# Products of probabilities with values for two heads at a time, in alternating column halves of TensorE

## The chip, the cores and the metric

The kernel runs on one core of a Trainium2 chip. A core has five engines that work beside each other: TensorE (PE, matrix products; its weight loads are shown apart as PEld), VectorE (DVE), ScalarE (ACT), GpSimd (POOL) and SyncE (SP, which here issues DMA transfers). TensorE writes only to PSUM, eight banks of 2 KB per partition; the other engines read from there. The metric is the device time of one execution in microseconds (us), the median of three runs.

## The reference

A forward pass of 512 tokens (and 256 context tokens) of width 1024 through two layers of a first block, each a mixer and a mixture of experts, and one layer of a second block. The change touches two mixers only. What they compute there is softmax attention with heads of 64:

```python
def gqa_attend(qb, k, v):
    s = jnp.einsum('bqhgd,bkhd->bhgqk', qb, k).astype(jnp.float32) * ATTN_SCALE
    p = jax.nn.softmax(s, -1)
    return jnp.einsum('bhgqk,bkhd->bqhgd', p.astype(v.dtype), v)
...
def sink_attend(qb, k, v, sink, valid=None):
    ...
    p = jax.nn.softmax(jnp.concatenate([s, sk], -1), -1)[..., :-1]
    return jnp.einsum('bhgqk,bkhd->bqhgd', p.astype(v.dtype), v)
...
def row_block(a):
    ...
    p = jax.nn.softmax(jnp.concatenate([s_nb, s_cx], -1), -1).astype(v.dtype)
    return (jnp.einsum('bhqk,bqkhd->bqhd', p[..., :n_nb], v_nb)
            + jnp.einsum('bhqk,bkhd->bqhd', p[..., n_nb:], vc))
```

The first is the first mixer's (2 groups of 4 heads, each group with one set of keys and values), the second the second mixer's window attention (2 groups of 4 heads again), the third its neighbourhood attention (8 heads). The last product of each, of the probabilities `p` with the values `v`, is what the change rearranges.

## The kernel before

All of it is float32. The projections and scores use float32r operands, split into a high and a low part; the transposes of the probabilities and their products with the values are plain float32, and in the trace each of these products leaves two matmul records.

**Stages that matter here.** In the first mixer (`mixer_ab`) `attend_gqa(u)` runs for the groups u = 4 and 5: 6 blocks of 128 queries times 4 heads. The two context blocks come first (256 keys, 2 blocks of keys), then four blocks with 768 keys (6 blocks of keys). In the second mixer (`mixer_cd`) `attend_window(g)` runs for g = 0 and 1: 4 blocks times 4 heads with 4 or 5 blocks of keys. Then `attend_near(u)` runs for u = 0 to 3: 4 column groups times 2 heads with 4 blocks of keys.

**One head.** `front` makes the scores `s` on TensorE (in PSUM, tag "s"), the negated maximum `nm` on VectorE, the exponential `p` and its sum on ScalarE, and multiplies `p` by the reciprocal of the sum on VectorE. `back` transposes `p` block by block on TensorE into `t` (PSUM, tag "aux"), three blocks to a tile, ScalarE copies each tile to `pT` in SBUF, and TensorE multiplies the 64 columns of values, as stationary operand, with each block of `pT` and accumulates in `po` (tag "aux" again). A head's 64 columns of values use half of the array's columns: the lower half for even heads, the upper for odd ones, and the result stands in partitions 0 to 63 or 64 to 127 of `po`. ScalarE then copies these 64 partitions to `oT`; where the result is the last one (u = 5, near u = 3) ScalarE writes the high part `oh` and VectorE the low part `ol`.

**What sets the order.** Each attention stage is a generator that yields once per head, and `both` takes steps of a second generator in between: the projection of the next group, or for u = 5 products of modulation rows and for near u = 3 nothing. Heads overlap by one: the front of the next head is written before the back of this one (near u = 3: three ahead). From this text a scheduler sets a fixed order for each engine, and every engine then goes through its list in that order. The tags "s", "mm" and "aux" of PSUM have two buffers each, so a new "aux" tile waits until the one before the last has been read.

**Other users.** The mixture of experts does its products in the same half-array form: `up` (line 1555) writes its two 64-row halves of `u` in turn, and the state products `pz` of the second block (line 2119) go to the two halves by turns too.

Of the kernel before, what the change touches and what calls it, by code (L numbers as in the profile page):

```python
# [13 lines left out]
F32 = mybir.dt.float32  # L14
# [3 lines left out]
AF = mybir.ActivationFunctionType  # L18
# [5 lines left out]
P = 128  # L24
# [146 lines left out]
class Kern:  # L171
# [276 lines left out]
    def scores_softmax(self, ap, ps, q, khl, k0, kn, tag, bufs):  # L448
# [12 lines left out]
        nc.scalar.activation(p[:, :kn], s[:, :kn], AF.Exp, bias=nm, accum_out=den)  # L461
        return p, den

    def probs_T(self, ap, ps, p, kn):
        nc = self.nc
        nk = kn // P
        pT = ap.tile([P, 6, P], F32, tag="pT", name="pT")
        for a in range(0, nk, 3):
            n = min(3, nk - a)
            t = ps.tile([P, 3, P], F32, tag="aux", name="t")  # L470
            for j in range(n):
                self.transpose(t[:, j], p[:, (a + j) * P:(a + j + 1) * P])
            nc.scalar.activation(pT[:, a:a + n], t[:, :n], AF.Copy)
        return pT
# [35 lines left out]
    def mixer_ab(self, atp, then):  # L510
        nc, tc, A, cp = self.nc, self.tc, self.A, self.cp
        NT, NB = NLAT + NCTX, 6
        with ExitStack() as es:
# [143 lines left out]
            def attend_diff(u):  # L657
                Q, Kh, Kl, V = ready[u]
                O = None
                oss = sp.tile([P, NB], F32, tag="oss", name="oss")  # L660

                def front(b):
                    k0, kn = keys(b)
                    (p0, d0), (p1, d1) = (self.scores_softmax(ap, ps, Q[:, c, b * P:(b + 1) * P], (Kh[:, c], Kl[:, c]), k0, kn,
                                                              f"p{c}", 2 - c) for c in range(2))
                    r0 = ap.tile([P, 1], F32, tag="r0", name="r0")
                    r1 = ap.tile([P, 1], F32, tag="r1", name="r1")
                    nc.vector.reciprocal(r0, d0)
                    nc.vector.tensor_scalar(p0[:, :kn], p0[:, :kn], r0, None, op0=OP.mult)
                    nc.vector.reciprocal(r1, d1)  # L670
                    nc.vector.tensor_mul(r1, r1, nlam)
                    nc.vector.scalar_tensor_tensor(p0[:, :kn], p1[:, :kn], r1, p0[:, :kn], op0=OP.mult, op1=OP.add)  # L672
                    return p0

                def back(b, p):
                    k0, kn = keys(b)
                    pT = self.probs_T(ap, ps, p, kn)
                    po = ps.tile([P, 512], F32, tag="aux", name="po")
                    for j in range(kn // P):
                        nc.tensor.matmul(po[:, :P], pT[:, j], V[:, k0 // P + j], start=j == 0, stop=j == kn // P - 1)  # L680
                    nc.scalar.activation(O[:, b], po[:, :P], AF.Copy)
                    nc.scalar.activation(po[:, P:2 * P], po[:, :P], AF.Square, accum_out=oss[:, b:b + 1])

                def norm():
                    v = sp.tile([P, NB], F32, tag="ov", name="ov")
                    nc.vector.tensor_scalar(v, oss, 1.0 / P, 1e-6, op0=OP.mult, op1=OP.add)
                    r = self.rsqrt(sp, v, NB)
                    for b in range(NB):
                        nc.vector.tensor_scalar_mul(O[:, b], O[:, b], r[:, b:b + 1])

                def out():
                    for b0 in (0, 3):
                        t = ps.tile([P, 3, P], F32, tag="aux", name="t")
                        for b in range(3):
                            self.transpose(t[:, b], O[:, b0 + b])
                        nc.scalar.activation(oT[:, u, b0 * P:(b0 + 3) * P], t, AF.Copy, scale=subg)

                p = front(0)
                while late:
                    late.pop(0)()  # L700
                O = sp.tile([P, NB, P], F32, tag="O", name="O", bufs=1)
                for b in range(NB):
                    nxt = front(b + 1) if b + 1 < NB else None
                    yield
                    back(b, p)
                    p = nxt
                late.extend((norm, out))

            def attend_gqa(u):
                Q, Kh, Kl, V = ready[u]  # L710
                order = (4, 5, 0, 1, 2, 3)

                def front(i):
                    b, h = order[i // 4], i % 4
                    k0, kn = keys(b)
                    p, den = self.scores_softmax(ap, ps, Q[:, h, b * P:(b + 1) * P], (Kh[:, 0], Kl[:, 0]), k0, kn, "p0", 2)
# [5 lines left out]
                def back(i, p):  # L722
                    b, h = order[i // 4], i % 4
# [6 lines left out]
                    rows, ch, tok = slice(o0, o0 + 64), 4 + (u - 4) * 2 + h // 2, slice(b * P, (b + 1) * P)  # L730
                    if u == 4:
                        nc.scalar.activation(oT[rows, ch, tok], po[rows, :P], AF.Copy)
                    else:
                        self.split(o[0][rows, ch, tok], o[1][rows, ch, tok], po[rows, :P])

                p = front(0)
                while late:
                    late.pop(0)()
                for i in range(4 * NB):
                    nxt = front(i + 1) if i + 1 < 4 * NB else None  # L740
                    yield
                    back(i, p)
                    p = nxt
                    if u == 5 and i % 4 == 0:
                        self.split(o[0][:, i // 4], o[1][:, i // 4], oT[:, i // 4])

            def last():
                yield from self.mod_rows(1, (1, 0), st, mp, ps, "mm", late=self.late)
# [31 lines left out]
    def mixer_cd(self, atp, then):  # L780
# [3 lines left out]
        with ExitStack() as es:  # L784
# [56 lines left out]
            def softmax(s, s0, s1, sinkcol, tag="p"):  # L841
                nm = ap.tile([P, 1], F32, tag="nm", name="nm", bufs=4)
                nc.vector.tensor_reduce(nm, s[:, s0:s1], axis=AX.X, op=OP.max, negate=True)
                if sinkcol is not None:
                    nc.vector.tensor_scalar(nm, nm, nsink[:, sinkcol:sinkcol + 1], None, op0=OP.min)
                p = ap.tile([P, 640], F32, tag=tag, name="p")
# [10 lines left out]
            def values(p, V, o0, wide=False):  # L857

                n = len(V)
                pT = ap.tile([P, 5, P], F32, tag="pT", name="pT")  # L860
# [7 lines left out]
                po = ps.tile([P, 512], F32, tag="aux", name="po")  # L868
                for j in range(n):
                    nc.tensor.matmul(po[o0:o0 + 64, :P], V[j], pT[:, j], start=j == 0, stop=j == n - 1)  # L870
                return po[o0:o0 + 64, :P]

            def project_window(g, Ws=()):
                QK = qp.tile([P, 3584], FR, tag="QK", name="QK")
# [32 lines left out]
            def attend_window(g):  # L907
# [18 lines left out]
                def back(i, p):  # L926
                    b, h = divmod(i, 4)
                    o0 = (h % 2) * 64
                    po = values(p, [V[:, j] for j in [*range(max(0, b - 1), min(4, b + 2)), 4, 5]], o0)
                    nc.scalar.activation(oT[o0:o0 + 64, g * 2 + h // 2, b * P:(b + 1) * P], po, AF.Copy)  # L930

                yield from piped(16, front, back)

            def project_near(u):
                c0 = u * P
# [54 lines left out]
            def attend_near(u):  # L990
# [19 lines left out]
                def back(i, p):  # L1010
                    g, h = divmod(i, 2)
                    hs = slice(h * 64, (h + 1) * 64)
                    po = values(p, [VW[:, g, 0, hs], VW[:, g, 1, hs], VX[:, 0, hs], VX[:, 1, hs]], h * 64, u == 3)
                    to = lambda t: t[hs, 4 + u, :NLAT].rearrange("p (r g i) -> p g r i", g=4, i=16)[:, g]
                    po = po.rearrange("p (r i) -> p r i", i=16)
                    if u < 3:
                        nc.scalar.activation(to(oT), po, AF.Copy)
                    else:
                        self.split(to(o[0]), to(o[1]), po)
                        if i < 7:  # L1020
                            self.split(o[0][:, i, :NLAT], o[1][:, i, :NLAT], oT[:, i])
# [1249 lines left out]

RAWS = 7

ORDER = [g * 8 + i for i in range(8) for g in range(4)]
# [81 lines left out]
```

## Time and profile before

| | us |
|---|---|
| median of 3 runs | 3471.41 |
| lowest, highest | 3470.51, 3473.18 |
| the profiled execution, whole | 3476.67 |
| its span, first to last instruction | 3474.9 |

The profile is of one execution. Its page gives each engine's busy time, and 40 slices of the span with the share of each engine in tenths. The first mixer's attention over u = 4 and 5 lies at 363 to 537 us, the second mixer's window and neighbourhood attention at 1365 to 1652 us. The trace can be asked for stretches, for lines of the kernel and for single instructions; the rows that are used stand two sections on. A matmul's record is longer than its place in the stream: matmuls are pipelined and a record includes the way through the array, so the pitch from start to start is the price of one, and a busy TensorE isn't one at its peak.

### The profile page before, as it was taken

What the parts mean: (1) busy time and instruction counts of PE and PEld (TensorE: products, weight loads), DVE (VectorE), ACT (ScalarE), POOL (GpSimd) and SP (SyncE); (2) the same over time, 40 slices, a digit from 0 to 9 for tenths busy, and PEclk for the clock granted to TensorE, in tenths of its full rate; (3) what the DMA queues carried; (4) which work ended last, traced back from release to release, by engine and by line L of the source; (5) the groups of instructions that cost most, each with busy time, mean ns of one, the idle gap of its engine ahead of it and who ended that gap; (6) DMA issues with size and microseconds to landing.
All of it is one profiled execution on the core that took longest, in us unless ns stands there. A gap on an engine that the chain in (4) does not pass through costs nothing. (4 is left out here: it accounts for less than half of the span.)

```text
span 3474.9 us, 50552 instructions
## 1 busy us (share of the span) xinstructions
PE 3146.0 (91%) x19045; PEld 2289.0 (66%) x19045; DVE 1479.0 (43%) x3317; ACT 1038.0 (30%) x2243; POOL 546.3 (16%) x533
## 2 busy tenths in 40 slices
PE   7999999799999938999799999569999999979998
PEld 3677767555555526887655555258798888858887
DVE  5578665521111147655622112154533333365533
ACT  4355562111111114655211111023223332233321
POOL 1101002141211111011232121220022210010000
PEclk9999999799999978999899999879999999989999
DMA  7433142699999641111499999552121212423332
GB/s 249 153 98 108 53 155 98 278 398 416 416 416 415 274 135 49 30 54 55 168 381 366 399 416 402 230 157 73 54 75 49 67 55 91 148 77 97 97 127 73
DMA packets 273506, 647.72 MB, mean 186 GB/s; under 512 B 58210, under 2 KB 176370, under 8 KB 223042
## 3 DMA queue, kind: packets, MB, share of 16 engines
q1 hardware_dynamic: 245522, 602.04, 46.5%
q0 software_dynamic: 26608, 38.36, 3.6%
q8 instruction: 187, 3.06, 0.4%
q10 hardware_dynamic: 1088, 3.42, 0.3%
q14 instruction: 101, 0.83, 0.1%
HBM read 670.51 MB, written 47.61 MB: 207 GB/s over the span
## 5 line engine op out<-in xcount | busy, mean ns | idle before, releaser
L1555 PE MATMUL u<-raw,xs 128*64 128x256 f32 x5376 | 602.1, 383 | 4.5 <-DMA raw<-in_k_w 4.1
L1555 PEld LDWEIGHTS u<-raw,xs 128*64 128x64 f32 x5376 | 381.9, 138 | 205.7 <-issue 15.0
L235 DVE TENSOR_TENSOR wl<-raw,wh 128x2048 fp32r<-128x2048 f32 (+4 forms) x176 | 273.7, 1561 | 430.1 <-ACT wh L234 428.6
L234 ACT ACTIVATE wh<-raw 128x2048 fp32r<-128x2048 f32 (+3 forms) x180 | 239.4, 1335 | 436.6 <-PE pm L229 187.9
L228 PE MATMUL pm<-hTh,wh 128*128 128x512 f32 x872 | 344.2, 395 | 1.9 <-DVE hTl L235 1.4
L230 PE MATMUL pm<-hTh,wl 128*128 128x512 f32 x872 | 340.9, 391 | 1.1 <-DVE wl L235 1.1
L229 PE MATMUL pm<-hTl,wh 128*128 128x512 f32 x872 | 341.2, 391 | 0.0
L1575 PE MATMUL y<-raw,gs 128*64 128x512 f32 x1344 | 305.0, 600 | 4.6 <-ACT gs L1570 2.1
L1560 DVE TENSOR_TENSOR sg<-sg,u 128x256 f32<-128x256 f32 x132 | 55.0, 420 | 498.5 <-PEq L1608 263.2
L1590 POOL DMA_INDIRECT y_d<-ys,rt_si x128 | 127.4, 995 | 716.9 <-issue 274.9
L228 PE MATMUL pm<-wh,aTh 128*128 128x384 f32 (+2 forms) x576 | 206.9, 360 | 8.0 <-ACT aTh L444 8.0
L230 PE MATMUL pm<-wh,aTl 128*128 128x384 f32 (+2 forms) x576 | 203.3, 353 | 4.0 <-POOL aTl L445 3.6
L1575 PEld LDWEIGHTS y<-raw,gs 128*64 128x64 f32 x1344 | 91.3, 137 | 171.8 <-issue 162.1
L229 PE MATMUL pm<-wl,aTh 128*128 128x384 f32 (+2 forms) x576 | 201.1, 350 | 2.1 <-DVE wl L235 2.1
L1559 ACT ACTIVATE sg<-u 128x256 f32<-128x256 f32 x132 | 50.6, 383 | 469.4 <-PE u L1555 298.0
L228 PEld LDWEIGHTS pm<-hTh,wh 128*128 128x128 f32 x872 | 163.6, 188 | 37.5 <-DVE hTl L235 1.8
L230 PEld LDWEIGHTS pm<-hTh,wl 128*128 128x128 f32 x872 | 163.3, 187 | 36.1 <-DVE wl L235 1.5
L229 PEld LDWEIGHTS pm<-hTl,wh 128*128 128x128 f32 x872 | 163.6, 188 | 34.4
L258 PE MATMUL t<-ident,p 128*128 128x128 f32 x704 | 127.5, 288 | 6.2 <-DVE p L672 1.1
L228 PEld LDWEIGHTS pm<-wh,aTh 128*128 128x128 f32 x576 | 115.4, 200 | 18.1 <-ACT aTh L444 11.2
L230 PEld LDWEIGHTS pm<-wh,aTl 128*128 128x128 f32 x576 | 115.0, 200 | 12.0 <-issue 4.9
L1582 DVE SCALAR_TENSOR_TENSOR ys<-y,rt_sw,gate 128x512 f32<-128x512 f32 x64 | 46.6, 749 | 178.2 <-PE y L1575 91.2
(557 smaller groups left out, 5583.9 us busy)
## 6 DMA issues: line engine op xcount, KB each, us to landing
raw<-in_k_w SPq DMA_DIRECT2D x408, 1024.0 KB
raw<-in_mod_w SPq DMA_DIRECT2D x192, 256.0 KB
raw<-in_w_in SPq DMA_DIRECT2D x16, 1024.0 KB
raw<-in_w_in SPq DMA_DIRECT2D x24, 512.0 KB
raw<-in_w_gate SPq DMA_DIRECT2D x12, 1024.0 KB
raw<-in_w_ff_gate SPq DMA_DIRECT2D x11, 1024.0 KB
raw<-in_w_ff_up SPq DMA_DIRECT2D x11, 1024.0 KB
raw<-in_w_ff_down SPq DMA_DIRECT2D x11, 1024.0 KB
```

The source lines that it names most:

```text
L228: nc.tensor.matmul(out, lh, rh, start=start, stop=False)
L229: nc.tensor.matmul(out, lh, rl, start=False, stop=False)
L230: nc.tensor.matmul(out, ll, rh, start=False, stop=stop)
L234: self.nc.scalar.activation(h, x, AF.Copy)
L235: (sub or self.nc.vector).tensor_sub(l, x, h)
L258: self.nc.tensor.transpose(out, in_, self.ident[:k, :k])
L1555: nc.tensor.matmul(pu[c][i][64 * n:64 * n + 64], xs[:, k, tok], w[:, k % 4, n * 256:(n + 1) * 256], start=k == 0, stop=k == KC - 1)
L1559: nc.scalar.activation(sg[c], pu[c][0], AF.Silu)
L1560: nc.vector.tensor_mul(sg[c], sg[c], pu[c][1])
L1575: nc.tensor.matmul(py[c][64 * n:64 * n + 64], gs[:, c, k % 2, k // 2], W[k // 2][:, k % 2, n * 512:(n + 1) * 512], start=k == 0, stop=k == 3)
L1582: nc.vector.scalar_tensor_tensor(y, py[c], sw, gate, op0=OP.mult, op1=OP.mult)
L1590: nc.gpsimd.indirect_dma_start(out=y_rows, out_offset=bass.IndirectOffsetOnAxis(ap=si, axis=0), in_=y, in_offset=None, bounds_check=4 * nt ...
```

## The change

The products of two heads are made together. `paired` replaces `piped` and the loop of `attend_gqa`: it keeps two fronts ahead, transposes one head per step (`turn`, `turned`, `probs_T`), and after each second head calls `back` with both transposed sets. The new `values` goes through the blocks of keys and issues for each block one product for the lower half and one for the upper half, both into one `po` tile, of which the lower 64 partitions belong to one head and the upper 64 to the other. So one copy (or one `oh` and one `ol`) of 128 partitions takes the place of two of 64. The tiles `pT` get 3 buffers in the first mixer (before 2) and 2 in the second as before; `p` alternates between two tags in `attend_gqa` with two buffers each, and has 3 buffers in the second mixer; near u = 3 goes from three fronts ahead to two.

```diff
+def paired(n, front, turn, back):
+
+    x, t = [front(i) for i in range(2)], []
+    for i in range(2 * n):
+        if i + 2 < 2 * n:
+            x.append(front(i + 2))
+        yield
+        t.append(turn(x.pop(0), i // 2))
+        if i % 2:
+            back(i // 2, t)
+            t = []
...
+    def values(self, po, parts):
+
+        n = len(parts[0][0])
+        for j in range(n):
+            for i, (V, pT) in enumerate(parts):
+                self.nc.tensor.matmul(po[64 * i:64 * i + 64], V[j], pT[:, j], start=j == 0, stop=j == n - 1)
...
-        pT = ap.tile([P, 6, P], F32, tag="pT", name="pT")
+        pT = ap.tile([P, 6, P], F32, tag="pT", name="pT", bufs=PT0)
...
-                                                              f"p{c}", 2 - c) for c in range(2))
+                                                              f"p{c}", 2) for c in range(2))
...
-                    pT = self.probs_T(ap, ps, p, kn)
                     po = ps.tile([P, 512], F32, tag="aux", name="po")
-                    o0 = (h % 2) * 64
-                    for j in range(kn // P):
-                        nc.tensor.matmul(po[o0:o0 + 64, :P], V[:, k0 // P + j, 0:64], pT[:, j], start=j == 0, stop=j == kn // P - 1)
+                    v = [V[:, k0 // P + j, 0:64] for j in range(kn // P)]
+                    self.values(po[:, :P], [(v, x) for x in pT])
...
-                        nc.scalar.activation(oT[rows, ch, tok], po[rows, :P], AF.Copy)
+                        nc.scalar.activation(oT[:, ch, tok], po[:, :P], AF.Copy)
...
+                yield from paired(2 * NB, front_, turn, back)
...
-                yield from piped(16, front, back)
+                yield from paired(8, front, lambda p, i: turned(p, len(blocks(i // 2))), back)
...
-                yield from piped(8, front, back, 3 if u == 3 else 1)
+                yield from paired(4, front, lambda p, i: turned(p, 4, u == 3), back)
...
+PT0, PT1, PP = 3, 2, 3
```

**What moves in the order.** The scheduler makes a new order in these stages; before the first of them and after the last one the orders are the same. TensorE has the same instructions as before, among them 496 products of probabilities with values. ScalarE has 56 copies fewer and VectorE 16 subtractions fewer. On TensorE the 496 products stand in runs, between which other products or transposes stand. Their number, by stage:

| stage | products | runs before | runs now |
|---|---|---|---|
| u = 4 | 112 | 38 | 18 |
| u = 5 | 112 | 30 | 22 |
| window 0 | 72 | 23 | 8 |
| window 1 | 72 | 22 | 10 |
| near 0 | 32 | 8 | 4 |
| near 1 | 32 | 9 | 4 |
| near 2 | 32 | 8 | 4 |
| near 3 | 32 | 7 | 7 |
| sum | 496 | 145 | 77 |

TensorE in stage u = 5, blocks with 768 keys, before. `s` are scores, `t` transposes of one head's `p`, `po` the products.

```order
L258 MATMUL t<-ident,p_5778 128x128 x3
L729 MATMUL po<-pT,V 64x128 x3
L455 MATMUL s<-QK 128x256
L456 MATMUL s<-QK 128x256
L729 MATMUL po<-pT,V 64x128 x3
L258 MATMUL t<-ident,p_5813 128x128 x3
L455 MATMUL s<-QK 128x512
L258 MATMUL t<-ident,p_5813 128x128 x3
L729 MATMUL po<-pT,V 64x128 x6
```

The same place now, one pair of heads (`p_5680` and `p_5704`):

```order
L271 MATMUL t<-ident,p_5680 128x128 x3
L468 MATMUL s<-QK 128x512
L469 MATMUL s<-QK 128x512
L468 MATMUL s<-QK 128x256
L469 MATMUL s<-QK 128x256
L271 MATMUL t<-ident,p_5680 128x128 x3
L271 MATMUL t<-ident,p_5704 128x128 x3
L468 MATMUL s<-QK 128x512
L469 MATMUL s<-QK 128x512
L271 MATMUL t<-ident,p_5704 128x128 x3
L482 MATMUL po<-pT,V 64x128 x7
L468 MATMUL s<-QK 128x256
```

The products of one head, six in one run or in two of three, have become the twelve of a pair in runs of 7 and 5 (or of 12), with the scores of the heads to come between the transposes.

ScalarE at the same place before: `p` is the exponential, `pT` the copy of a tile of transposes, `oh` that of a result.

```order
L461 ACTIVATE p_5745,den<-s,nm 128x768
L234 ACTIVATE oh<-po 64x128
L473 ACTIVATE pT<-t 128x384 x2
L461 ACTIVATE p_5778,den<-s,nm 128x768
L234 ACTIVATE oh<-po 64x128
```

And now:

```order
L247 ACTIVATE oh<-po 128x128
L493 ACTIVATE pT<-t 128x384
L474 ACTIVATE p_5743,den<-s,nm 128x768
L493 ACTIVATE pT<-t 128x384 x2
L474 ACTIVATE p_5767,den<-s,nm 128x768
L493 ACTIVATE pT<-t 128x384
L247 ACTIVATE oh<-po 128x128
```

Per pair one `oh` of 128 partitions has taken the place of two of 64, and an exponential now stands ahead of the last `pT` of the pair.

TensorE in stage near 0 before, in the middle of the next projection (`pm`):

```order
L228 MATMUL pm<-wh,aTh 128x384
L870 MATMUL po<-pT,VW 64x128 x2
L870 MATMUL po<-pT,VX 64x128 x2
L229 MATMUL pm<-wl,aTh 128x384
L230 MATMUL pm<-wh,aTl 128x384
```

and now:

```order
L243 MATMUL pm<-wh,aTl 128x256
L482 MATMUL po<-pT,VW 64x128 x4
L482 MATMUL po<-pT,VX 64x128 x4
L241 MATMUL pm<-wh,aTh 128x256
L242 MATMUL pm<-wl,aTh 128x256
```

Runs of four have become half as many runs of eight.

## Rows read from the trace of the kernel before

**Rows 1.** The page: busy time of TensorE; its busy tenths in 40 slices.

```profile
PE 3146.0 (91%) x19045; PEld 2289.0 (66%) x19045; DVE 1479.0 (43%) x3317; ACT 1038.0 (30%) x2243; POOL 546.3 (16%) x533
...
PE   7999999799999938999799999569999999979998
```

**Rows 2.** Windows: the eight stages (u 4, 5; window 0, 1; near 0 to 3).

```profile
core 0: us, PE busy (x) PEld busy (x) DVE busy (x) ACT busy (x) POOL busy (x), PEclk, DMA share, GB/s
363.50:461.40 97.90, 96.29 (x653) 69.35 (x655) 62.54 (x201) 54.04 (x148) 7.77 (x10) 0.97 0.25 79
461.40:536.50 75.10, 70.64 (x491) 49.73 (x490) 44.29 (x107) 45.85 (x122) 6.65 (x11) 1.00 0.38 133
1365.00:1427.30 62.30, 59.93 (x388) 48.67 (x386) 40.85 (x128) 37.10 (x119) 4.79 (x6) 0.95 0.08 24
1427.30:1495.00 67.70, 67.49 (x456) 56.88 (x454) 42.19 (x127) 43.95 (x149) 0.56 (x2) 1.00 0.12 34
1495.00:1542.30 47.30, 47.23 (x312) 40.40 (x311) 27.14 (x66) 27.00 (x97) 6.92 (x7) 1.00 0.21 59
1542.30:1586.30 44.00, 43.96 (x292) 37.68 (x291) 22.21 (x56) 24.25 (x90) 5.64 (x6) 1.00 0.10 26
1586.30:1630.50 44.20, 42.70 (x280) 36.03 (x279) 22.28 (x57) 25.32 (x93) 5.38 (x4) 1.00 0.28 95
1630.50:1651.50 21.00, 16.29 (x116) 12.73 (x116) 13.96 (x37) 12.59 (x33) 2.85 (x2) 1.00 0.01 2
```

**Rows 3.** Tile `po`: the products and their weight loads (ns shortest/median/longest, first and last start).

```profile
L729 PEld LDWEIGHTS po<-pT,V x448: 132/137/231, 363.7 to 535.5; 128*64 128x64 f32 x150
L729 PE MATMUL po<-pT,V x448: 272/273/476, 363.7 to 535.6; 128*64 128x128 f32 x150
...
L870 PE MATMUL po<-pT,V x288: 272/273/476, 1365.5 to 1494.4; 128*64 128x128 f32 x144
...
L870 PE MATMUL po<-pT,VW x128: 272/273/324, 1501.6 to 1650.1; 128*64 128x128 f32 x128
...
L870 PE MATMUL po<-pT,VX x128: 272/273/323, 1502.1 to 1650.6; 128*64 128x128 f32 x128
```

**Rows 4.** Timeline of TensorE in stage u = 5: start, length, instruction, records.

```profile
504.26 0.49 PE L258 MATMUL t<-ident,p 128*128 128x128 f32 x3
504.68 1.52 PE L729 MATMUL po<-pT,V 128*64 128x128 f32 x12
506.13 0.55 PE L258 MATMUL t<-ident,p 128*128 128x128 f32 x3
506.44 0.36 PE L456 MATMUL s<-QK 128*128 128x256 f32 x1
...
507.80 0.87 PE L729 MATMUL po<-pT,V 128*64 128x128 f32 x6
508.60 0.39 PE L456 MATMUL s<-QK 128*128 128x256 f32 x1
```

**Rows 5.** Timeline of TensorE in the second block: products in alternating halves.

```profile
2491.03 0.88 PE L2119 MATMUL pz<-V,qkT 128*64 128x128 f32 x12
2491.84 0.49 PE L2109 MATMUL po<-V,ST 128*128 128x128 f32 x2
```

**Rows 6.** Timeline of TensorE in the mixture of experts: accumulating products in alternating halves.

```profile
800.46 7.13 PE L1555 MATMUL u<-raw,xs 128*64 128x256 f32 x64
```

**Rows 7.** Groups by line and shape, 500 to 536 us, ScalarE: busy, mean ns | idle before.

```profile
L473 ACT ACTIVATE pT<-t 128x384 f32<-128x384 f32 x22 | 10.7, 490 | 7.4 <-PE t L258 7.4
...
L461 ACT ACTIVATE p<-s,nm 128x768 f32<-128x768 f32 x9 | 8.1, 898 | 0.1
...
L234 ACT ACTIVATE oh<-po 64x128 fp32r<-64x128 f32 x12 | 3.3, 271 | 7.1 <-PE po L729 6.6
...
L461 ACT ACTIVATION_READ_ACCUMULATOR p<-s,nm 128x1 f32 x9 | 1.8, 197 | 0.0
```

**Rows 8.** Windows: a stretch of stage window 0 at the lower clock.

```profile
1419.70:1426.50 6.80, 6.69 (x28) 5.34 (x29) 2.21 (x3) 2.55 (x8) 0.00 (x0) 0.50 0.59 174
```

More of the change, by code (lines that the diff above doesn't have):

```diff
@@ L715, in front @@
                     k0, kn = keys(b)
-                    p, den = self.scores_softmax(ap, ps, Q[:, h, b * P:(b + 1) * P], (Kh[:, 0], Kl[:, 0]), k0, kn, "p0", 2)
+                    p, den = self.scores_softmax(ap, ps, Q[:, h, b * P:(b + 1) * P], (Kh[:, 0], Kl[:, 0]), k0, kn, f"p{i % 2}", 2)
                     r0 = ap.tile([P, 1], F32, tag="r0", name="r0")
@@ L720, in front, with turn, back, front_ @@
                     return p
-                def back(i, p):
-                    b, h = order[i // 4], i % 4
+                def turn(p, i):
+                    return self.probs_T(ap, ps, p, keys(order[i // 2])[1])
+                def back(i, pT):
+                    b, h = order[i // 2], i % 2 * 2
                     k0, kn = keys(b)
-                    pT = self.probs_T(ap, ps, p, kn)
                     po = ps.tile([P, 512], F32, tag="aux", name="po")
-                    o0 = (h % 2) * 64
-                    for j in range(kn // P):
-                        nc.tensor.matmul(po[o0:o0 + 64, :P], V[:, k0 // P + j, 0:64], pT[:, j], start=j == 0, stop=j == kn // P - 1)
-                    rows, ch, tok = slice(o0, o0 + 64), 4 + (u - 4) * 2 + h // 2, slice(b * P, (b + 1) * P)
+                    v = [V[:, k0 // P + j, 0:64] for j in range(kn // P)]
+                    self.values(po[:, :P], [(v, x) for x in pT])
+                    ch, tok = 4 + (u - 4) * 2 + h // 2, slice(b * P, (b + 1) * P)
                     if u == 4:
-                        nc.scalar.activation(oT[rows, ch, tok], po[rows, :P], AF.Copy)
+                        nc.scalar.activation(oT[:, ch, tok], po[:, :P], AF.Copy)
                     else:
[L734 to L745, printed above, removed]
+                        self.split(o[0][:, ch, tok], o[1][:, ch, tok], po[:, :P])
+                        if i % 2 == 0:
+                            self.split(o[0][:, i // 2], o[1][:, i // 2], oT[:, i // 2])
+                def front_(i):
+                    p = front(i)
+                    if i == 0:
+                        while late:
+                            late.pop(0)()
+                    return p
+                yield from paired(2 * NB, front_, turn, back)
             def last():
@@ L845, in softmax @@
                     nc.vector.tensor_scalar(nm, nm, nsink[:, sinkcol:sinkcol + 1], None, op0=OP.min)
-                p = ap.tile([P, 640], F32, tag=tag, name="p")
+                p = ap.tile([P, 640], F32, tag=tag, name="p", bufs=PP if tag == "p" else 2)
                 den = ap.tile([P, 2], F32, tag="den", name="den", bufs=4)
@@ L855, in softmax, with turned @@
                 return p
-            def values(p, V, o0, wide=False):
-                n = len(V)
-                pT = ap.tile([P, 5, P], F32, tag="pT", name="pT")
+            def turned(p, n, wide=False):
+                pT = ap.tile([P, 5, P], F32, tag="pT", name="pT", bufs=PT1)
                 step = 4 if wide else 3
@@ L867, in values @@
                     nc.scalar.activation(pT[:, a:a + m], t[:, :m], AF.Copy)
[L868 to L871, printed above, removed]
+                return pT
+            def values(pTs, V):
+                po = ps.tile([P, 512], F32, tag="aux", name="po")[:, :P]
+                self.values(po, list(zip(V, pTs)))
+                return po
             def project_window(g, Ws=()):
@@ L924, in front, with blocks, back @@
                     return softmax(s, s0, 768, 4 * g + h)
[L926 to L930, printed above, removed]
-                yield from piped(16, front, back)
+                def blocks(b):
+                    return [*range(max(0, b - 1), min(4, b + 2)), 4, 5]
+                def back(i, pTs):
+                    b, h = divmod(i, 2)
+                    po = values(pTs, 2 * [[V[:, j] for j in blocks(b)]])
+                    nc.scalar.activation(oT[:, g * 2 + h, b * P:(b + 1) * P], po, AF.Copy)
+                yield from paired(8, front, lambda p, i: turned(p, len(blocks(i // 2))), back)
             def project_near(u):
@@ L1008, in front, with back @@
                     return softmax(s, 0, 512, None, "qk" if u == 3 and i % 2 else "p")
[L1010 to L1015, printed above, removed]
+                def back(g, pTs):
+                    v = [[t[:, a, h * 64:(h + 1) * 64] for t in (VW[:, g], VX) for a in range(2)] for h in range(2)]
+                    po = values(pTs, v).rearrange("p (r i) -> p r i", i=16)
+                    to = lambda t: t[:, 4 + u, :NLAT].rearrange("p (r g i) -> p g r i", g=4, i=16)[:, g]
                     if u < 3:
@@ L1019, in back @@
                         self.split(to(o[0]), to(o[1]), po)
-                        if i < 7:
-                            self.split(o[0][:, i, :NLAT], o[1][:, i, :NLAT], oT[:, i])
-                yield from piped(8, front, back, 3 if u == 3 else 1)
+                        for i in (2 * g, 2 * g + 1):
+                            if i < 7:
+                                self.split(o[0][:, i, :NLAT], o[1][:, i, :NLAT], oT[:, i])
+                yield from paired(4, front, lambda p, i: turned(p, 4, u == 3), back)
             pc = ps.tile([P, 2, 2, KC], F32, tag="aux", name="pc")
```

## The prediction

> **What bounds the kernel now.** I read the page first. TensorE is busy for 91% of the span, and in the slices that hold the two mixers' attention (the 5th to 7th and nearly all of the 17th to 19th) it stands at 9 tenths [rows 1]. So time that TensorE is spared there should mostly come off the end. Then the windows over the eight stages that the change touches [rows 2]: 459.5 us together, TensorE busy 444.5, VectorE 275, ScalarE 270. In six of them TensorE is busy for 96% or more and the next, VectorE or ScalarE, for 55 to 66%: these are TensorE's. In u = 5 it is 94% with ScalarE at 61%, and in near 3, which has no second work beside it, 78% with VectorE at 66%: there the chain of one head shows through.
>
> The products of probabilities with values are 448 + 288 + 128 + 128 = 992 records, two for each of 496 products [rows 3].
>
> **What one product costs.** A record lasts 273 ns [rows 3], but what counts is the pitch. In the timeline a run of 12 records starts at 504.68 and the next instruction at 506.13: 1.45 us. A run of 6 takes 508.60 - 507.80 = 0.80 us [rows 4]. So a record costs (1.45 - 0.80)/6 = 0.108 us and a run 0.15 us beside. Going in costs too: from three transposes to a product 0.42 us, from three transposes to a score 0.31 us [rows 4], so 0.11 more. A run costs 0.26 us, whatever its length.
>
> The same shape in alternating halves is in this trace already: twelve records of `pz` with the next instruction 0.81 us later [rows 5]. With the same 0.15 for the run this is 0.055 us per record. Those don't accumulate over several products; the 64 records of `u` do, with 256 columns, at (7.13 - 0.38)/63 = 0.107 us [rows 6], which is half of what 256 columns would take at 0.108 per 128. So 0.055 is taken, a gain of 0.053 us per record. Its bounds are 0 (the halves don't overlap) and this.
>
> The Trainium skill ("TensorE: Matmul & The Clock Gate", part 3, what overlaps and what doesn't) says that a weight load hides behind a running product only when it goes to other rows of the array. The two halves share their rows, so by that rule the loads would show; rows 5 speak against it.
>
> **The sum on TensorE.** 992 records x 0.053 = 52.6 us. The order has 77 runs in place of 145, 68 x 0.26 = 17.7 us. Together 70 us: u = 4 17.1 (224 records, 20 runs fewer), u = 5 14.0 (224, 8), window 0 11.5 (144, 15), window 1 10.7 (144, 12), near 0 to 2 4.4 + 4.7 + 4.4 (64 each; 4, 5, 4), near 3 3.4 (64, none).
>
> **What of it reaches the end.**
> *u = 4, windows, near 0 to 2.* Take the saving off the stage and look at who comes next. In u = 4 81 us remain with 62.5 of VectorE, in window 0 51 with 41, in window 1 57 with 44 of ScalarE, in the near stages 43, 39 and 40 with 27, 24 and 25 [rows 2]. TensorE still has the most work in each, and the next projection to fill its waits. I take 15, 10, 9.5 and 12.5 of the 17.1, 11.5, 10.7 and 13.5: about a tenth is lost where VectorE comes to four fifths of the stage and a fixed order meets a wait.
>
> *u = 5.* The projection isn't there to fill. A head with 768 keys takes 36 us / 11 = 3.27 us now (22 copies `pT`, two per head) [rows 7]. In the new order the chain of a pair runs over ScalarE: one `oh` 0.27, four `pT` 4 x 0.49, two exponentials with their read-out 2 x (0.90 + 0.20), 4.43 us in all [rows 7]. The last `pT` has to be done before the last five products, and these before `oh`: 0.26 + 10 x 0.055 = 0.81. That is 5.24 per pair, 2.62 per head, a gain of 0.65 for each of 16 heads = 10.4; the 8 heads with 256 keys give 32 records x 0.053 = 1.7. I take 11, less than TensorE's 14.0.
>
> *near 3.* Three engines at 60 to 78% of 21 us and nothing to fill: with two fronts ahead in place of three it can lose as well as gain. I take 0.5, bounds -3 and 3.4.
>
> *Copies.* 56 copies fewer on ScalarE at 0.27 = 15 us, and 16 subtractions on VectorE. In the stages of TensorE they lay under its work and count nothing; in u = 5 they are in the chain above.
>
> *Waits that are added.* A pair's first product waits for the second head's transposes, and behind it on TensorE stand the scores of the next head. In the new order the scores of the heads to come stand ahead of it, so the wait is covered but for the start of a stage: 8 stages, about 0.2 us each, -1.5. More buffers for `p` in the first mixer's differential attention (two in place of one) change no order there; 0.
>
> *Transfers.* The next weights and the experts' streams are issued as buffers come free at the end of each mixer, so they move forward with it; 0.
>
> Sum: 15 + 11 + 10 + 9.5 + 12.5 + 0.5 - 1.5 = 57 us. The profiled execution took 3476.7 us, 5.3 above the median; with 57 off it is 3420, and the median goes from 3471.4 to **3414 us**.
>
> **The rivals.**
> *The copies bind everywhere (the gain halves).* "aux" has two buffers, and a pair needs five tiles in turn. In the new order an exponential stands ahead of the pair's last `pT` on ScalarE. If TensorE waits for half of it with its read-out, 0.55 us, in the 40 pairs of u = 4, the windows and near 0 to 2, 22 us go: gain 35, 3436 us. For it: VectorE and ScalarE rise to 60 to 80% of those stages. Against: the projections are there to fill, and before, with the same two buffers, TensorE was idle for 3% over the eight stages [rows 2].
> The Trainium skill ("TensorEngine Tiling (Array Packing)", PSUM bottleneck) warns of this: tiling makes TensorE faster but not the emptying of PSUM, and the copies may become the bound.
>
> *All of it arrives.* 70 us, and the stretch at half clock in window 0, 1419.7 to 1426.5 [rows 8], goes as well: TensorE's busy 6.7 us there would take 3.4 at full clock. Gain 73, 3398 us. Against: u = 5 and near 3 have little to fill with.
>
> *The halves don't overlap.* If the second half's products wait for the first's, or each load of 0.137 us [rows 3] stands open so that two records take 0.107 + 0.137 = 0.244, 0.122 each, only the runs gain: 17.7, or with open loads 17.7 - 992 x 0.014 = 4. That is 3454 to 3467 us; that the change doesn't do what it says ends there too. Rows 5 and 6 speak against it. By the page's rule on loads it would be the latter.
>
> *Slower: each pair waits for its own chain.* If nothing stood between the second head's transposes and the pair's products, TensorE would wait in all 56 pairs for an exponential and a `pT`, 1.10 + 0.49 = 1.59 us: 89 us against 70, so 3490 us. From 70/56 = 1.25 us per pair on it is a loss. Only the last two pairs of u = 5 stand so in the shown order.
>
> **How the numbers follow.** Forecast 3414 (own range 3404 to 3426) 0.63, halved gain 3436 0.22, all of it 3398 0.08, no overlap 0.04, slower 0.03. From 3400 to 3440 the first two are in, and the rest, 0.15, is left out. A measurement of this kernel can tell 0.2%, 7 us, from no change. Faster by more: 0.63 + 0.22 + 0.08 and the upper half of the fourth, 0.95; the same 0.02; slower 0.03.
>
> **What would show it.** In the new profile the products' pitch should be 0.055 us in runs of 7 to 12 (a run of 24 records, next instruction 1.5 us later); u = 4 near 83 us, u = 5 near 64, the windows near 52 and 58, near 0 to 2 near 43, 40 and 40, near 3 at 20 to 22. A pair of u = 5 should take 5.2 us with ScalarE hardly idle. TensorE's waits on `pT` growing in the stages with a projection would be the halved gain; a pitch of 0.1 the missing overlap. Stretches at half clock that weren't there before, 3.4 us each, would be a cost that I haven't counted.

## The result and the profile after

The changed kernel takes 3412.64 us (median of 4 runs, 3406.39 to 3417.14); the kernel before takes 3471.76 us beside it (3470.51 to 3473.18). The ratio is 0.9827, with a 95% interval of 0.9812 to 0.9842: 59 us or 1.7% faster. Measured twice more, beside the kernel before each time, it took 3409.76 and 3410.16 us against 3471.35 and 3471.89, 62 us less. The forecast was 3414 in a range of 3400 to 3440, and faster.

The profiled execution of the changed kernel took 3411.29 us, its span 3409.5. Its span is 65.4 us shorter than that shown before, a little more than the medians differ: the execution profiled before lay 5.3 us above the median of its three runs (3471.41), this one 1.4 below.

The page's line of TensorE and its slices, to be held against [rows 1]:

```profile
PE 3080.5 (90%) x19045; PEld 2239.7 (66%) x19045; DVE 1471.9 (43%) x3301; ACT 1018.6 (30%) x2187; POOL 546.9 (16%) x533
...
PE   7999999799999937998799999389999999979998
```

TensorE has the same 19045 records and is busy 65.5 us less, the whole of the gain in the span. ScalarE has 56 instructions fewer and VectorE 16. The slices of the two mixers are still at 9 tenths: what TensorE was spared came off the end.

The eight stages again, in the order of [rows 2], each up to its last product (columns: stretch, its length, busy time and instructions of each engine, granted clock, DMA share, GB/s):

```profile
core 0: us, PE busy (x) PEld busy (x) DVE busy (x) ACT busy (x) POOL busy (x), PEclk, DMA share, GB/s
363.50:446.10 82.60, 80.62 (x647) 57.29 (x648) 62.59 (x210) 49.40 (x133) 6.92 (x10) 1.00 0.29 93
446.10:510.50 64.40, 61.48 (x493) 41.11 (x492) 40.00 (x95) 40.55 (x109) 6.53 (x11) 1.00 0.45 157
1343.00:1392.60 49.60, 45.94 (x374) 38.96 (x374) 39.46 (x122) 32.59 (x108) 4.70 (x6) 0.97 0.05 15
1392.60:1451.00 58.40, 57.92 (x459) 49.81 (x458) 42.03 (x128) 41.64 (x142) 0.57 (x2) 1.00 0.15 42
1451.00:1494.00 43.00, 42.86 (x317) 37.69 (x316) 26.82 (x67) 26.07 (x93) 6.79 (x7) 1.00 0.29 80
1494.00:1533.00 39.00, 38.87 (x293) 34.29 (x292) 22.38 (x56) 23.30 (x86) 5.62 (x7) 1.00 0.11 29
1533.00:1572.00 39.00, 37.01 (x277) 32.11 (x277) 22.68 (x59) 24.04 (x89) 5.02 (x5) 1.00 0.30 101
1572.00:1589.80 17.80, 13.97 (x120) 10.38 (x119) 12.28 (x32) 11.69 (x29) 2.92 (x3) 1.00 0.04 17
```

Length before less length now gives what each stage won: 15.3, 10.7, 12.7, 9.3, 4.3, 5.0, 5.2 and 3.2, together 65.7 us. The start of window 0 is the one that I had to choose, since its products begin at another point of the work than before. From the last product of u = 5 to the last of window 0 it is 891.2 us before, 882.2 here and 878.9 and 878.7 in the two other profiles of the changed kernel, so that window 0 is worth 9 to 12.5 us by these. In the windows and near 0 to 2 TensorE is still busy for 93 to nearly 100% of the stage, and VectorE and ScalarE have come to 57 to 80%: no copy has become the bound.

Not all of the 65.7 us is the change's own work. The profile before has stretches at half clock in two of these stages: 6.8 us in window 0 [rows 8], and this one at the head of u = 4 (granted clock 0.52):

```profile
363.50:368.60 5.10, 4.97 (x20) 3.76 (x20) 2.97 (x9) 2.65 (x11) 0.81 (x1) 0.52 0.00 0
```

At full clock it would be some 2.4 us shorter, an estimate from its length and clock. In the changed kernel u = 4 has no such stretch and window 0 one of half the length, so that 2.4 + 1.7 = 4.1 us of the stages' gain are clock, which the forecast didn't count. The other profile with the old u = 4 (second mixer alone) has 3.2 us at half clock there as well, and none of the ten profiles with a new one has any; that the new order takes it away isn't shown.

The products themselves (shortest/median/longest in ns, first and last start):

```profile
L482 PE MATMUL po<-pT,V x736: 272/273/473, 364.5 to 1450.5; 128*64 128x128 f32 x184
...
L482 PE MATMUL po<-pT,VW x128: 272/273/324, 1465.4 to 1588.5; 128*64 128x128 f32 x128
```

With 128 more of `po<-pT,VX` they are the same 992 records as in [rows 3], and a record still lasts 273 ns. What changed is the pitch. The timeline of TensorE (start, length, instruction, records) shows a run of 12 products in stage u = 4 and one of 8 in window 1, each with the instruction behind it:

```profile
400.18 1.53 PE L482 MATMUL po<-pT,V 128*64 128x128 f32 x24
401.64 0.55 PE L271 MATMUL t<-ident,p 128*128 128x128 f32 x3
...
1407.88 1.09 PE L482 MATMUL po<-pT,V 128*64 128x128 f32 x16
1408.90 0.44 PE L242 MATMUL pm<-wl,aTh 128*128 128x384 f32 x1
```

24 records in 401.64 - 400.18 = 1.46 us and 16 in 1.02: (1.46 - 1.02)/8 = 0.055 us per record and 0.14 for the run. Before, 12 records took 1.45 [rows 4].

### The profile page after: what moved, and what is told of

Read it like the earlier page. It is cut to its first block, busy times and chain, and to the rows that moved or that the text cites. A ratio compares the mean times of both kernels' runs of the same rounds, so it can differ in the third digit from the quotient of the medians.

```text
span 3409.5 us, 50444 instructions
## 1 busy us (share of the span) xinstructions
PE 3080.5 (90%) x19045; PEld 2239.7 (66%) x19045; DVE 1471.9 (43%) x3301; ACT 1018.6 (30%) x2187; POOL 546.9 (16%) x533
## 5 line engine op out<-in xcount | busy, mean ns | idle before, releaser
L242 PEld LDWEIGHTS pm<-hTl,wh 128*128 128x128 f32 x872 | 163.6, 188 | 34.5
L242 PEld LDWEIGHTS pm<-wl,aTh 128*128 128x128 f32 x576 | 114.7, 199 | 5.8 <-issue 3.1
```

Of the source, the lines that this page charges most:

```text
L242: nc.tensor.matmul(out, lh, rl, start=False, stop=False)
```

## The experiments

The theory is that of the forecast: the overlap of the two halves (0.053 us for each of 992 records) and fewer runs (0.26 us each) make the gain, in the stages of TensorE; in u = 5 a chain over ScalarE sets the pace. The rivals are that the gain is something else of the rewriting (order, fewer copies, buffers), or that the pace of u = 5 is set elsewhere.

**The two halves not by turns.** All products of the lower half, then all of the upper half:

```diff
-        for j in range(n):
-            for i, (V, pT) in enumerate(parts):
+        for i, (V, pT) in enumerate(parts):
+            for j in range(n):
```

> Pairs of heads as in the change, one result tile and one copy of 128 partitions per pair, but all products of the lower half are issued before those of the upper half. The order has 68 runs of products (145 before the change, 77 with it). Theory (the overlap of the halves is what pays): 992 records at 0.108 in place of 0.055 us give back 52.6 us, the nine runs fewer keep 2, so about 50 us above the changed kernel, near 3460. Rival (longer runs, fewer copies and two fronts ahead are what pays): within 10 us of the changed kernel, 3410 to 3425.

Measured: 3436.35 us (3432.06 to 3447.57), ratio 0.9898 [0.9882, 0.9915]. That is 26.6 us slower than the changed kernel measured beside it (3409.76), and half of what the loss of the overlap was to cost: a miss. The timeline of TensorE in u = 5 tells why:

```profile
502.36 2.45 PE L482 MATMUL po<-pT,V 128*64 128x128 f32 x24
504.75 0.55 PE L271 MATMUL t<-ident,p 128*128 128x128 f32 x3
```

24 records take 2.39 us, between the 1.46 of alternating halves and the 2.74 that 0.15 + 24 x 0.108 gives. The windows over this run, in steps of some 0.45 us, have it in the number of weight loads (PEld; one that crosses the edge counts twice):

```profile
502.82:503.28 0.46, 0.46 (x6) 0.46 (x5) 0.44 (x1) 0.46 (x1) 0.00 (x0) 1.00 0.00 0
503.28:503.72 0.44, 0.44 (x10) 0.44 (x9) 0.18 (x1) 0.44 (x2) 0.00 (x0) 1.00 0.00 0
503.72:504.18 0.46, 0.46 (x9) 0.46 (x5) 0.36 (x2) 0.04 (x1) 0.00 (x0) 1.00 0.00 0
```

Nine loads in the middle stretch where its neighbours have five: the first four records of the upper half (from 503.29) run beside the last four of the lower half. So the order of this program doesn't take the overlap away, only shortens it to four records at the seam: 2.77 - 2.39, some 0.38 us per run (2.77 is measured in the next experiment). Of its 68 runs 46 have such a seam; most of the others hold products of one head alone. In the changed kernel, on the other side, 42 products have no partner in the other half, since they stand in runs of odd length; they have no overlap to lose, 42 x 0.11 = 4.6 us (the 0.11 is read below, at u = 5). With 9 runs fewer than the changed kernel's 77 the loss should be 52.6 - 4.6 - 46 x 0.38 - 9 x 0.26 = 28; measured 26.6. This sum was made after the result. The program was the wrong one to remove the overlap with; the number that it gave fits the price of the overlap all the same.

**One half only.** The products of both heads go to the lower half of the array, head after head, into two column ranges of `po`, in u = 4, the windows and near 0 to 2; u = 5 and near 3 stay. Two copies take the place of one, since the results stand in the same partitions.

```diff
-        for j in range(n):
-            for i, (V, pT) in enumerate(parts):
-                self.nc.tensor.matmul(po[64 * i:64 * i + 64], V[j], pT[:, j], start=j == 0, stop=j == n - 1)
+        for j, i in [(j, i) for i in range(2) for j in range(n)] if low else [(j, i) for j in range(n) for i in range(2)]:
+            V, pT = parts[i]
+            out = po[0:64, P * i:P * i + P] if low else po[64 * i:64 * i + 64, :P]
+            self.nc.tensor.matmul(out, V[j], pT[:, j], start=j == 0, stop=j == n - 1)
```

> Pairs as in the change, but in u = 4, the windows and near 0 to 2 both heads of a pair go to the lower half of the array's columns, one after the other, side by side in the result tile; two copies of 64 partitions follow. u = 5 and near 3 stay as in the change. 704 records cannot overlap, 67 runs of products. Theory (engine starts the other half's products ahead of the end of this half's, which the run without alternation showed in its last 8 records, and in one half it can't): 704 x 0.053 = 37 us back, 10 runs fewer 2.6, so 34 above the changed kernel, near 3445. Rival (the earlier run lost only 27 us because long runs are cheaper per record anyway): 704 of 992 of that, 19 us, near 3430.

Measured: 3444.69 us (3440.73 to 3446.67), 0.992 [0.9902, 0.9938], which is 34.5 us over the changed kernel beside it (3410.16). A run of 12 products, and the instruction behind it, in u = 4:

```profile
384.54 2.83 PE L483 MATMUL po<-pT,V 128*64 128x128 f32 x24
387.31 0.55 PE L271 MATMUL t<-ident,p 128*128 128x128 f32 x3
```

2.77 us in place of 1.46. The 704 records of these stages at 0.053 would be 37.3, less 10 x 0.26 = 2.6 for ten runs fewer (67): 34.7 (32.9 if the 16 products that have no partner in these stages of the changed kernel are taken off). So the overlap is what these stages owe most of their gain to, at the price that [rows 4, 5] gave. What is left of the gain in them fits the runs: u = 4 goes from 97.9 to 88.7 us here with no overlap at all, 6.8 us without the 2.4 of clock, and it has 25 runs fewer, 6.5 us. Window 1 and near 0 to 2 together are 5.9 us shorter than before with 27 runs fewer, 0.22 each. The order and the fronts ahead are new in these stages too, so that a run's price isn't shown by itself.

```profile
362.20:450.90 88.70, 86.63 (x635) 67.16 (x634) 61.46 (x206) 51.59 (x141) 7.02 (x10) 1.00 0.26 82
```

**Each mixer alone.** The first kernel has the change in the first mixer only, the second in the second only (shown are the calls).

```diff
 (first mixer alone)
-                yield from paired(8, front, lambda p, i: turned(p, len(blocks(i // 2))), back)
+                yield from piped(16, front, back)
...
-                yield from paired(4, front, lambda p, i: turned(p, 4, u == 3), back)
+                yield from piped(8, front, back, 3 if u == 3 else 1)
```

```diff
 (second mixer alone)
-                yield from paired(2 * NB, front_, turn, back)
+                for i in range(4 * NB):
+                    nxt = front(i + 1) if i + 1 < 4 * NB else None
+                    yield
+                    back(i, p)
+                    p = nxt
```

> Pairs in the first mixer alone; window and neighbourhood attention as before the change. Forecast: the first mixer is worth 15 + 11 = 26 us less some 0.4 for the fills, so 3446. If the trace's shift is right and the two mixers are independent, 26 to 28. Rival (what is gained early is given back in the stages between, whose clock the first mixer's end shifts): 20 or less, above 3451.

> Pairs in the second mixer alone; the first as before the change. Forecast: 10 + 9.5 + 12.5 + 0.5 less 1.2 for the fills = 31 us, so 3440. The shift in the trace of the changed kernel says 40 between 1340 and 1590 us, so 3432. Together with the run on the first mixer alone the gains should add up to 59 if nothing is shared.

> The changed kernel itself, as the measure for the three runs beside it. 3412.6 us median before; 3406 to 3417 is expected again, the product records of a run at a pitch of 0.055 us.

Measured against 3471.35: the first alone 3443.78 (3441.91 to 3447.28), 0.9926 [0.991, 0.9943], 27.6 us; the second alone 3436.53 (3433.72 to 3440.86), 0.99 [0.9884, 0.9917], 34.8 us; both 3409.76 (3407.16 to 3412.86), 0.9826 [0.981, 0.9842], 61.6 us. 27.6 + 34.8 = 62.4: the parts add up to 1 us, where executions of one of these kernels differ by 5 to 7, and nothing that the first mixer wins is seen to be taken back later. The first mixer's 27.6 stands beside 26 of the forecast (15 + 11), the second's 34.8 beside 32.5; it lies between the 31 and the 40 that were expected ahead of the run.

**Who sets the pace in u = 5.** The last transposed copy of a pair moves from ScalarE to VectorE:

```diff
-            nc.scalar.activation(pT[:, a:a + n], t[:, :n], AF.Copy)
+            if last and a:
+                nc.vector.tensor_copy(pT[:, a:a + n], t[:, :n])
+            else:
+                nc.scalar.activation(pT[:, a:a + n], t[:, :n], AF.Copy)
```

> In stage u = 5 the copy of a pair's last tile of transposes goes to VectorE in place of ScalarE, where it stood behind an exponential. Theory of the prediction (the chain of a pair runs over ScalarE: 4.43 us and the last products): a pair takes 0.5 us less, 4.8 in place of 5.3, and with 8 pairs the kernel gains 3 to 4 us. Rival (TensorE's own list is the chain there: 5.31 us per pair in the trace without a wait of over 0.3 us): a pair stays at 5.2 to 5.3 us and the kernel within 1.5 us of the changed one.

> The changed kernel again, as the measure for the three runs beside it: 3410 to 3413 us.

Measured: 3409.87 us (3406.74 to 3413.59), 0.9825 [0.981, 0.984], against 3410.16 (3408.52 to 3417.33) for the changed kernel: no difference that the executions could show. The runs of 7 products in two pairs of this kernel:

```profile
480.16 1.09 PE L482 MATMUL po<-pT,V 128*64 128x128 f32 x14
...
485.43 1.09 PE L482 MATMUL po<-pT,V 128*64 128x128 f32 x14
```

A pair takes 485.43 - 480.16 = 5.27 us with 0.49 taken off ScalarE, where it took 5.31 (below). The chain over ScalarE, on which the forecast's 5.24 rested, doesn't set the pace. What does is read from TensorE's timeline of one pair of the changed kernel:

```profile
490.65 0.55 PE L271 MATMUL t<-ident,p 128*128 128x128 f32 x3
490.95 0.48 PE L468 MATMUL s<-QK 128*128 128x512 f32 x1
491.26 0.39 PE L469 MATMUL s<-QK 128*128 128x512 f32 x1
491.50 0.28 PE L468 MATMUL s<-QK 128*128 128x256 f32 x1
491.61 0.28 PE L469 MATMUL s<-QK 128*128 128x256 f32 x1
491.83 0.87 PE L271 MATMUL t<-ident,p 128*128 128x128 f32 x6
492.71 0.50 PE L468 MATMUL s<-QK 128*128 128x512 f32 x1
493.05 0.40 PE L469 MATMUL s<-QK 128*128 128x512 f32 x1
493.29 0.49 PE L271 MATMUL t<-ident,p 128*128 128x128 f32 x3
493.71 1.09 PE L482 MATMUL po<-pT,V 128*64 128x128 f32 x14
494.72 0.39 PE L468 MATMUL s<-QK 128*128 128x256 f32 x1
494.95 0.28 PE L469 MATMUL s<-QK 128*128 128x256 f32 x1
495.16 0.87 PE L482 MATMUL po<-pT,V 128*64 128x128 f32 x10
495.96 0.55 PE L271 MATMUL t<-ident,p 128*128 128x128 f32 x3
```

From transposes to the same transposes it is 495.96 - 490.65 = 5.31 us, and no row has idle time ahead of it. ScalarE over the same pair, every instruction (in brackets the idle time ahead of it):

```profile
491.29 0.49 ACT L493 ACTIVATE pT<-t 128x384 f32<-128x384 f32 x1 [0.26 <-PE t L271]
491.68 0.90 ACT L474 ACTIVATE p<-s,nm 128x768 f32<-128x768 f32 x1
492.46 0.20 ACT L474 ACTIVATION_READ_ACCUMULATOR p<-s,nm 128x1 f32 x1
492.55 0.87 ACT L493 ACTIVATE pT<-t 128x384 f32<-128x384 f32 x2
493.30 0.92 ACT L474 ACTIVATE p<-s,nm 128x768 f32<-128x768 f32 x1
494.08 0.23 ACT L474 ACTIVATION_READ_ACCUMULATOR p<-s,nm 128x1 f32 x1
494.17 0.52 ACT L493 ACTIVATE pT<-t 128x384 f32<-128x384 f32 x1
496.06 0.28 ACT L247 ACTIVATE oh<-po 128x128 fp32r<-128x128 f32 x1 [1.38 <-PE po L482]
```

It waits 1.38 us for the products and 0.26 for transposes, so that its own work fills 5.31 - 1.64 = 3.67 us of the pair. The last copy ends at 494.69 and the products that read it start at 495.16, 0.47 us later, so that the chain has up to 0.47 us to spare there. TensorE's own list is full, and part of it is the split of the twelve products: the run of 7 takes 494.72 - 493.71 = 1.01 us, as much as a run of 8, and the run of 5 takes 0.80, as much as a run of 6. This fits a product that has no partner and takes the 0.22 us of two.

**The twelve in one run.** With the blocks of keys taken in reverse order in u = 5, a pair's products stand in one run; the last copy is on VectorE as above, and near 3 has three fronts ahead again (that alone is the next experiment).

```diff
-        for j in range(n):
-            for i, (V, pT) in enumerate(parts):
-                self.nc.tensor.matmul(po[64 * i:64 * i + 64], V[j], pT[:, j], start=j == 0, stop=j == n - 1)
+        for k in range(n):
+            j = n - 1 - k if down else k
+            for i, (V, pT) in [*enumerate(parts)][::-1 if down else 1]:
+                self.nc.tensor.matmul(po[64 * i:64 * i + 64], V[j], pT[:, j], start=k == 0, stop=k == n - 1)
```

> The kernel of e6 with, in the stage u=5, the block order of a pair turned round so that its 12 products stand in one run (none of 7 and 5), and the last transposed copy of a pair on VectorE; 65 runs in all where the changed kernel has 68 and more of them in u=5 alone. If TensorE pays for the split into 7 and 5 (entries of two runs, halves of unequal length), the cycle of a pair goes from 5.31 to 4.8 to 5.0 us and the stage from 64 to 60 to 62 us: about 3 us under e6, 3404 us. Rival: the one run waits for the last transposed copy of its pair, the cycle stays at 5.2 to 5.3 us and the time is that of e6, 3407 us.

(The changed kernel has 77 runs, not 68 as that text says.) Measured: 3405.44 us (3402.98 to 3406.0), 0.9801 [0.9788, 0.9815], the fastest of all, 4.3 to 7.2 us under the three medians of the changed kernel (its interval only touches theirs) and 1.7 under the kernel of the next experiment (3407.15; the intervals of the two overlap), where about 3 were forecast. Two pairs:

```profile
481.40 1.53 PE L483 MATMUL po<-pT,V 128*64 128x128 f32 x24 [0.28 <-ACT p L474]
...
486.31 1.53 PE L483 MATMUL po<-pT,V 128*64 128x128 f32 x24 [0.27 <-ACT p L474]
```

A pair takes 4.91 us in place of 5.31, and now it ends in a wait of 0.27 for ScalarE's exponential. That is what the theory asked of the trace (4.8 to 5.0), and the wait names who comes next. The stage, from the last product of u = 4 to its own last one, is 62.2 us, just outside the 60 to 62 of the forecast; it is 64.2 in the changed kernel, 63.7 in the next experiment, which leaves u = 5 alone, and 63.4 with the copy on VectorE and nothing else.

**Near 3 with three fronts ahead**, as before the change:

```diff
-                yield from paired(4, front, lambda p, i: turned(p, 4, u == 3), back)
+                yield from paired(4, front, lambda p, i: turned(p, 4, u == 3), back, 3 if u == 3 else 2)
```

> Neighbourhood stage u = 3 keeps three fronts ahead, as before the change, in place of two. Forecast: the stage has nothing to fill with, so one more head in flight may give up to 2 us; if the stage is set by VectorE and ScalarE, no change (within 1 us of the changed kernel).

Measured: 3407.15 us (3405.35 to 3408.15), 0.9813 [0.9798, 0.9827], 3.0 us under the changed kernel beside it, with intervals that overlap. The trace is clearer than the times: from the last product of near 2 to the last of near 3 it is 15.6 us, and 17.4 in the changed kernel and in both profiles of it taken again. TensorE's wait for transposed copies in near 3, first in the changed kernel and then here (us in total, times, longest):

```profile
PE po L482 <- ACT pT L886: 2.1, 6, 0.7
```

```profile
PE po L482 <- ACT pT L886: 0.7, 3, 0.3
```

The third front fills most of this wait: 1.4 of the 1.8 us.

**Without the added buffers.**

```diff
-PT0, PT1, PP = 3, 2, 3
+PT0, PT1, PP = 2, 2, 2
```

> The changed kernel with the old numbers of buffers for the transposed probabilities and the products (two of each). If the added buffers matter, the windows, where two heads' copies must stand ahead of a joint run, lose what they won (windows 22 us of gain): 3430 us. If TensorE's own work alone sets the windows, the order changes by a dozen more runs at 0.26 us, or 3 us: 3413 to 3416 us.

(The order has 80 runs, three more than the changed kernel's, not a dozen: 0.8 us. `p` in `attend_gqa` keeps its two tags of two buffers each.) Measured: 3418.29 us (3408.18 to 3421.01), 0.9844 [0.9829, 0.9859], against 3473.01. The median lies between the two forecasts and 6 to 9 us above those of the changed kernel, but the intervals overlap (the changed kernel's last one is [0.9811, 0.9848]), and the profiled execution is the fastest of the four, 3408.18. The first forecast, by which the windows lose their 22 us, falls: window 1, from the last product of window 0 to its own, takes 59.0 us here and 58.5 in the changed kernel.

```profile
1368.40:1375.20 6.80, 6.55 (x36) 5.24 (x35) 3.14 (x11) 2.46 (x8) 0.00 (x0) 0.50 0.01 2
...
1385.90:1444.90 59.00, 58.79 (x466) 50.79 (x464) 43.00 (x128) 41.68 (x141) 0.56 (x2) 1.00 0.17 48
```

The first row is a stretch at half clock in window 0, which makes that stage look longer; it is worth 3.4 us at most, and the profile of the changed kernel has one of half the length there. Whether the buffers are worth 1 us or several stays open.

## Why the prediction was right

**The price of a product** (0.055 us in place of 0.108) came from twelve `pz` of another part of the kernel [rows 5]. Runs of 16 and 24 in the changed kernel give 0.055. The kernel with one half shows it as a cause: 34.5 us where 34.7 are worked out from it. By the rule of the Trainium skill ("TensorE: Matmul & The Clock Gate", part 3), loads for the same rows of the array would have shown; here they don't, 24 loads of 0.137 us, 3.3 us in all, lie within 1.46 us.

**The price of a run** (0.26 us) fits where there is no overlap: 6.8 us for 25 runs fewer in u = 4, 5.9 for 27 in four other stages. It lacks one thing, that a run with an odd number of products costs as much as one with one product more. A run takes 0.15 us and 0.22 for each two products begun, one for each half: 1.47 for twelve, 1.03 for eight or seven, 0.81 for six or five, where 1.46, 1.02 and 1.01, and, for five, 0.80 were read. The prediction gave every record a partner. In the changed kernel's timeline 42 products have none, 12 of them in u = 4, 20 in u = 5, 4 in window 1 and 6 in near 3, so that TensorE's 70 us are some 66.

**Where the gain reaches the end.** u = 4 forecast 15, measured 15.3, and that is luck in part: 2.4 are clock, and 12.9 remain of the 17.1 by records and runs (15.8 without the products that have no partner); window 0 10 and 9 to 12.7, of which 1.7 are clock, since the stretch of 6.8 us at half clock [rows 8] has become one of 3.4:

```profile
1378.30:1381.70 3.40, 3.40 (x27) 3.19 (x27) 2.73 (x9) 1.80 (x6) 0.00 (x0) 0.50 0.03 7
```

Window 1 9.5 and 9.3; near 0 to 2 12.5 and 14.5. The tenth that I took off for waits in these stages wasn't lost in the near stages, and they won a little more than the 13.5 of their records and runs. The halved gain (3436) had little for it: over u = 4, the windows and near 0 to 2 TensorE is idle for 8.4 us by the two tables, 5.8 before, so that 2.6 were added where the rival had 22. In the windows and near 0 to 2 it waits for the copies of the transposes for 2.8 us in all (waits of TensorE from 1343 to 1572 us: total, times, longest):

```profile
PE po L482 <- ACT pT L886: 1.4, 4, 0.5
PE t L271 <- ACT pT L886: 1.4, 6, 0.4
```

**u = 5** was right by accident: 11 us forecast, 10.7 measured, 5.24 us per pair forecast, 5.31 measured, but not for the reason given. The step that failed reads "the chain of a pair runs over ScalarE". Freeing ScalarE by 0.49 changed nothing, and "ScalarE hardly idle", the sign named for it, didn't come: it is idle for 1.64 us in each pair. Two errors cancelled. The 4.43 us of ScalarE added up record lengths, which overlap there as they do on TensorE: from the exponential at 491.68 to the copies at 492.55 it is 0.87 us, not 1.10, and the two copies take 0.75, not 0.98. With the 3.67 us that were measured the chain would be 3.67 + 0.81 = 4.48. And TensorE itself pays for the split into 7 and 5 that the order showed. With two products of 0.11 us without a partner in each of the 10 pairs that are split (the small ones into 1 and 3, the last two pairs not) its 14.0 are 14.0 - 2.2 = 11.8. What sets the pace is TensorE's own list.

**near 3** is the term that was mis-sized: 0.5 forecast with bounds of -3 and 3.4 and a stage of 20 to 22 us, 3.2 and 17.8 measured. The loss by two fronts in place of three is there, 1.8 us by the experiment, but the pair with its single copy wins 4.9 with three fronts, more than TensorE's 3.4 by records: that with nothing to fill the shorter chain counts as well is a reading, and no run tests it by itself.

**The sum.** Stage by stage it is 62 to 66 us in the profiles, 58 to 62 without the 4.1 of clock, where 57 were forecast, and by the medians 59, 62 and 62. The forecast of 3414 is 1.4 us above the first median, 3412.64, and 4 above the two others. These are of one kernel, and outside the eight stages its executions differ by as much: the 882.2 and 878.9 us above lie between the mixers for the most part, and their difference of 3.3 us isn't in any of the stages. Both profiles have the same 139.9 us at half clock in this stretch, so the amount of it doesn't explain the difference; what does stays open.

## What to carry to other kernels

Where a product uses half of the array's columns, two of them that go to different halves by turns cost little more than one: 0.055 us per record in place of 0.108, by experiment 37 us for 704 records here (34.5 and the 2.6 for runs). Write them as close pairs and in runs with an even number of products: a run costs some 0.26 us here, and an unpaired product costs 0.11 us more than a paired one. Before an engine's chain is named as the pace of a stage, add up the busiest engine's own list for one cycle, by starts and not by record lengths: it took one timeline to see that it was full, and that ScalarE's 4.43 us were 3.67.

## What was not expected of the hardware

Two runs of products to different halves overlap at their seam without being written by turns: the upper half began when four records of the lower half were still to come, and 24 records took 2.39 us in place of 2.77. And a run of 7 products takes as long as one of 8 (1.01 and 1.02 us), a run of 5 as long as one of 6 (0.80, and 0.81 for the `pz` of [rows 5]).
